# The last two feed-forward blocks get a second input X with the norm's factors in it, and wide up products from the third pair on

## The chip, the cores and the metric

The kernel runs on one core of one Trainium2 chip. The metric is device time in microseconds (us) of one execution of the whole program. TensorE (PE in the profile) multiplies, VectorE (DVE) and ScalarE (ACT) do elementwise work, GpSimd (POOL) sets a few pad columns to zero, SyncE (SP) issues the transfers of the weights.

## What is computed

Four transformer layers of width 1024 on one short sequence: two layers on 272 positions (16 of them meta tokens), then two on 256. Each layer is a mixer and a feed-forward block (FFN). The change is in the FFN of the last two layers:

```python
def conv_glu_ffn(xn, w_up, conv_w, w_down):
    u = causal_dwconv_2(xn @ w_up, conv_w)          # w_up: 1024 x 5632, 3 taps, each channel
    g, val = jnp.split(u, 2, axis=-1)               # 2816 gate channels, 2816 value channels
    return (jax.nn.silu(g) * val) @ w_down          # w_down: 2816 x 1024

def rms_norm_2(x, g):
    y = xf * lax.rsqrt(jnp.mean(xf * xf, axis=-1, keepdims=True) + EPS)
    return (y * g.astype(jnp.float32)).astype(x.dtype)

x = x + conv_glu_ffn(rms_norm_2(x, ffn_norm[l]), ffn_w_up[l], ffn_conv_w[l], ffn_w_down[l])
```

In the first two layers only the gate half goes through the convolution.

## The kernel before

Activations lie transposed: 128 channels on the partitions, positions (T = 256 here) along the free axis, so `hv[0..7]` hold the 1024 channels. A product in full float32 is made of three products of rounded float32 ("fp32r"): every operand is split into a high and a low part, and hi·hi, hi·lo and lo·hi are summed in PSUM. For the activations that split is done once for each norm (`X`: a tile with [high | low] side by side, 512 columns). For the weights it is done for each tile of 128x1024 as it arrives: ScalarE writes `whi` (L257), VectorE subtracts to get `wlo` (L258).

The norm is pulled apart. `X` holds only x times the gain g. The factor of each position, rB, comes later (`Norm.factors`: squares, sums, a reciprocal root on VectorE, and a broadcast through TensorE), so that products can start before it is known, and each output is multiplied by rB when it leaves PSUM.

An FFN walks over 11 pairs. A pair is two gate outputs (`evg`) and two value outputs (`evu`) of 128 channels each. I call each such output a unit: U1 to U44 in an FFN, U1 to U4 being the first pair. A unit has 8 steps along the 1024 input channels. `mm3` has two forms of a step:

```python
        if ps.shape[1] == 2 * n:
            mm(ps.rearrange("p (a n) -> p a n", a=2), w[0], x, start=first, stop=False)
        else:
            mm(ps, w[0], hi, start=first, stop=False)
            mm(ps, w[0], lo, start=False, stop=False)
        mm(ps[:, :n], w[1], hi, start=False, stop=last)
```

The narrow form is three products of 256 columns. The wide form is one of 512 (whi against [high | low]) and one of 256, and leaves two halves in the PSUM bank that must still be added. Before, the last two FFNs (`both=True`) use the narrow form in all of gate and up; `down` uses the wide one. The FFN of the second layer (`both=False`) already uses the wide form for its value outputs: there ScalarE copies one half out (L405) and VectorE adds the other (L406).

A unit of the last two FFNs is evicted in `conv3`: VectorE multiplies PSUM by rB into `gu` or `vu` (L382), ScalarE scales by the first tap (L385), VectorE adds the two others (L386, L387). A gate unit then goes through Silu (L396, ScalarE). For a value unit VectorE multiplies by the gate (L410, `a`), and the result is split for `down` (`ax`, L257 and L258). So VectorE has 3 instructions for every unit, 2 more for a value unit and one `wlo` for every unit: 20 for a pair of the walk.

Each engine runs its instructions in one fixed order, which the tile framework's scheduler decides when the program is built. So an instruction that waits holds up all that stand behind it on its engine. Three buffers bind the engines to each other: `whi` and `wlo` have 4 buffers each (a unit takes one of each), the PSUM tag `d` has 3 banks (U4 needs the bank of U1), and the raw weights have 2 buffers of two units.

`tick` runs twice a unit, and each time advances every chain that was started (the norm's factors are such a chain).

Of the kernel before, what the change touches and what calls it, by code (L numbers as in the profile page):

```python
# [11 lines left out]
F32 = mybir.dt.float32  # L12
F32R = mybir.dt.float32r
I32 = mybir.dt.int32
AF = mybir.ActivationFunctionType
OP = mybir.AluOpType
# [3 lines left out]
P = 128  # L20
D = 1024
KT = D // P
NMETA = 16
SEQ = 256
T1 = NMETA + SEQ
# [106 lines left out]
class Norm:  # L132
# [1 line left out]


    def __init__(self, k, hv, g, segs, delay):
        self.k, self.hv, self.segs, self.delay = k, hv, segs, delay
        V, A = k.nc.vector, k.nc.scalar
        T = hv[0].shape[1]
        self.X = []  # L140
        for t in range(KT):
            x = k.st.tile([P, 2, T1], F32R, tag=f"x{t}", name=f"x{t}")[:, :, :T]
            xh, xl = x[:, 0, :], x[:, 1, :]
            A.activation(xh, hv[t], AF.Copy, scale=g[:, t:t + 1])
            V.scalar_tensor_tensor(xl, hv[t], g[:, t:t + 1], xh.bitcast(F32), OP.mult, OP.subtract)
            self.X.append(x)
        self._u = self._r = self._rB = None
        self.chain = self.factors()
        k.start(self.chain)
# [36 lines left out]
    u = property(lambda self: self.have("_u"))  # L186
# [4 lines left out]
class K:  # L191
# [174 lines left out]
    def ffn(self, hv, N, lead, w_up, conv, w_down, both, done=None):  # L366

        nc, V, A = self.nc, self.nc.vector, self.nc.scalar
        X = N.X
        TX = X[0].shape[2]  # L370
        T = TX - lead
        XU = [x[:, :, lead:] for x in X]
        hv = [t[:, lead:] for t in hv]
        with self.tc.tile_pool(name="ffn", bufs=2) as fp:
            acts = []
            wide = 2 if 2 * T <= 512 and not both else 1

            def conv3(ps, c, tag):
                n = ps.shape[1]
                u = fp.tile([P, 2 + T1], F32, tag=tag + "u", name=tag + "u")  # L380
                nc.gpsimd.memset(u[:, 0:2], 0.0)
                V.tensor_tensor(u[:, 2:2 + n], ps, N.rB, OP.mult)  # L382
                o = n - T
                y = fp.tile([P, T1], F32, tag=tag + "y", name=tag + "y")[:, :T]
                A.activation(y, u[:, o:o + T], AF.Copy, scale=conv(0, c))  # L385
                V.scalar_tensor_tensor(y, u[:, o + 1:o + 1 + T], conv(1, c), y, OP.mult, OP.add)  # L386
                V.scalar_tensor_tensor(y, u[:, o + 2:o + 2 + T], conv(2, c), y, OP.mult, OP.add)  # L387
                return y

            for p in range(NF // 2):  # L390
                G = {}

                def evg(m, ps, p=p, G=G):
                    y = conv3(ps, 2 * p + m, "g")
                    s = fp.tile([P, T1], F32, tag=f"s{m}", name=f"s{m}")[:, :T]
                    A.activation(s, y, AF.Silu)  # L396
                    G[m] = s

                def evu(m, ps, p=p, G=G):
                    if both:  # L400
                        y = conv3(ps, NF + 2 * p + m, "v")
                    else:
                        y = fp.tile([P, T1], F32, tag="vy", name="vy")[:, :T]
                        if wide == 2:
                            A.activation(y, ps[:, T:], AF.Copy)  # L405
                            V.tensor_tensor(y, ps[:, :T], y, OP.add)  # L406
                            ps = y
                        V.tensor_tensor(y, ps, N.rB[:, lead:], OP.mult)
                    a = fp.tile([P, T1], F32, tag="a", name="a")[:, :T]
                    V.tensor_tensor(a, y, G[m], OP.mult)  # L410
                    c = 2 * p + m
                    x = fp.tile([P, 2, T1], F32R, tag=f"ax{c}", name=f"ax{c}", bufs=1)[:, :, :T]
                    self.split(x[:, 0, :], x[:, 1, :], a)
                    acts.append(x)

                self.dense(w_up[p], X, evg)
                self.dense(w_up[NF // 2 + p], XU, evu, wide=wide)
            w = [self.pieces(w_down[m2], NF) for m2 in range(D // 256)]
            ahead = [next(w[0]), next(w[0])]
            self.evict()  # L420
            for m2 in range(D // 256):
                def ev(m, ps, m2=m2):
                    k = 2 * m2 + m
                    for o in range(0, ps.shape[1], T):
                        V.tensor_tensor(hv[k], ps[:, o:o + T], hv[k], OP.add)
                    if done:
                        done(k)
                self.dense_pair(w[m2], acts, ev, "ns"[m2 % 2], () if m2 else ahead)
# [26 lines left out]
def mixer1(k_, l, h, N, final, first=None):  # L455
    nc, V, A, G = k_.nc, k_.nc.vector, k_.nc.scalar, k_.nc.gpsimd
    mm, tr = nc.tensor.matmul, nc.tensor.transpose
# [17 lines left out]
    def tmp(name):  # L475
        return mp.tile([P, T1 + 4], F32, tag="tmp", name=name, bufs=7)
# [109 lines left out]
    def ev_conv(which, c0):  # L586
        def ev(m, ps):
            hh = c0 + m
            ci = {"q": 0, "k": 4, "v": 8}[which] + hh
            xp = tmp("xp")  # L590
            G.memset(xp[:, 0:3], 0.0)
            V.tensor_tensor(xp[:, 3:3 + T], ps, N.rB, OP.mult)
# [1036 lines left out]
```

## Time and profile before

| | us |
|---|---|
| median of 3 runs (1605.9 to 1612.46) | 1608.96 |
| the profiled execution's own time | 1609.75 |
| its span, first to last instruction | 1607.9 |
| gate and up of the third FFN, from U1's first product (1027.18) to down's first (1153.68) | 126.5 |
| the same of the last FFN (1414.72 to 1542.04) | 127.3 |

The 1.9 us between the span and the execution's own time lie outside the profile. The profile has one execution; a row of a timeline gives the start, the duration, the engine, the line and the tiles. Durations on TensorE are longer than the step from one product to the next, since products overlap in the array, so its pace is read from starts. The same holds for VectorE and ScalarE to a smaller degree.

### The profile page before, as it was taken

The numbers are of one execution on the slowest core, as the hardware profiler recorded it, in microseconds if no ns is written. First come the engines' busy times: TensorE is split into PE (matmuls) and PEld (weight loads), VectorE is DVE, ScalarE is ACT, GpSimd is POOL, SyncE is SP. The second block draws the span as 40 slices with busy tenths as digits, with TensorE's granted clock in tenths as the row PEclk, the third lists the DMA queues.
The fourth block names the chain that finished last, engine by engine and source line by source line (L and its number), as shares of the span: only waits on it lengthen the run. The fifth ranks groups of instructions, "written<-read, shape, count | busy, mean of one in ns | idle before, by whom it ended". The sixth has DMA issues, their size and how long they took to land.

```text
span 1607.9 us, 29362 instructions
## 1 busy us (share of the span) xinstructions
PE 1587.6 (99%) x11482; PEld 1477.2 (92%) x11482; DVE 1247.1 (78%) x2729; ACT 897.4 (56%) x1582; POOL 16.1 (1%) x170
## 2 busy tenths in 40 slices
PE   7999999999999999999999999999999999999998
PEld 7988999999999989999998988999988888899997
DVE  7798678888558886788986659999866777789974
ACT  6566555555445755656665547666554444556642
POOL 0000000000000000000000000000000000000000
PEclk9999999999999999999999999999999999999999
DMA  6423234555553323355555653455555455555553
GB/s 209 156 80 131 78 133 164 178 172 171 167 187 131 105 79 108 105 187 179 185 185 187 218 169 120 161 196 188 184 176 197 157 160 171 167 183 184 184 193 121
DMA packets 38441, 257.71 MB, mean 160 GB/s; under 512 B 4384, under 2 KB 6816, under 8 KB 9120
## 3 DMA queue, kind: packets, MB, share of 16 engines
q1 hardware_dynamic: 37440, 253.66, 46.8%
q8 instruction: 90, 1.47, 0.4%
q10 hardware_dynamic: 864, 2.18, 0.4%
q14 instruction: 47, 0.39, 0.1%
HBM read 254.78 MB, written 1.05 MB: 159 GB/s over the span
## 4 chain that ended last, share of the span: by engine, by line
PE 93%; DVE 4%; ACT 2%; issue 0%; DMA 0%; DVEq 0%; SPq 0%; ACTq 0%
PE psd L285 19%; PE psd L283 18%; PE psd L284 18%; PE pss L281 5%; PE psn L281 5%; PE psd L281 3%; PE pss L285 3%; PE psn L285 3%; PE stat L496 1%; PE psd L348 1%; PE psd L349 1%; PE psd L350 1%; DVE wlo L258 1%; PE psn L349 1%; PE psn L348 1%; PE psn L350 1%
## 5 line engine op out<-in xcount | busy, mean ns | idle before, releaser
L257 ACT ACTIVATE whi<-raw 128x1024 fp32r<-128x1024 f32 (+1 forms) x487 | 508.4, 1045 | 535.0 <-PE psd L284 278.2
L258 DVE TENSOR_TENSOR wlo<-raw,whi 128x1024 fp32r<-128x1024 f32 (+1 forms) x487 | 585.7, 1203 | 207.6 <-ACT whi L257 202.4
L285 PE MATMUL psd<-x,wlo 128*128 128x256 f32 (+2 forms) x2384 | 683.4, 287 | 0.8 <-DVE wlo L258 0.8
L283 PE MATMUL psd<-x,whi 128*128 128x256 f32 (+2 forms) x2208 | 642.7, 292 | 7.6 <-ACT whi L257 6.9
L284 PE MATMUL psd<-x,whi 128*128 128x256 f32 (+2 forms) x2208 | 631.4, 286 | 0.0
L285 PEld LDWEIGHTS psd<-x,wlo 128*128 128x128 f32 x2384 | 452.3, 190 | 4.2 <-DVE wlo L258 1.6
L283 PEld LDWEIGHTS psd<-x,whi 128*128 128x128 f32 x2208 | 419.9, 190 | 15.5 <-ACT whi L257 6.9
L284 PEld LDWEIGHTS psd<-x,whi 128*128 128x128 f32 x2208 | 421.1, 191 | 3.3 <-issue 1.7
L285 PE MATMUL psn<-ax,wlo 128*128 128x256 f32 (+1 forms) x352 | 99.2, 282 | 0.0
L285 PE MATMUL pss<-ax,wlo 128*128 128x256 f32 (+1 forms) x352 | 99.2, 282 | 0.0
L281 PE MATMUL psn<-ax,whi 128*128 128x512 f32 x264 | 92.3, 392 | 0.0
L281 PE MATMUL pss<-ax,whi 128*128 128x512 f32 x264 | 92.2, 392 | 0.0
L285 PEld LDWEIGHTS psn<-ax,wlo 128*128 128x128 f32 x352 | 66.2, 188 | 0.0
L285 PEld LDWEIGHTS pss<-ax,wlo 128*128 128x128 f32 x352 | 66.2, 188 | 0.0
L281 PE MATMUL psd<-x,whi 128*128 128x512 f32 x176 | 61.7, 393 | 0.0
L281 PEld LDWEIGHTS pss<-ax,whi 128*128 128x128 f32 x264 | 49.5, 188 | 11.3
L281 PEld LDWEIGHTS psn<-ax,whi 128*128 128x128 f32 x264 | 49.5, 188 | 11.3
L385 ACT ACTIVATE gy<-gu,prm 128x256 f32<-128x256 f32 (+1 forms) x88 | 43.8, 502 | 4.0 <-DVE gu L382 3.7
L387 DVE SCALAR_TENSOR_TENSOR gy<-gu,prm,gy 128x256 f32<-128x256 f32 (+1 forms) x88 | 42.6, 487 | 1.7
L386 DVE SCALAR_TENSOR_TENSOR gy<-gu,prm,gy 128x256 f32<-128x256 f32 (+1 forms) x88 | 42.4, 485 | 0.9 <-ACT gy L385 0.9
L382 DVE TENSOR_TENSOR gu<-psd,rB 128x256 f32<-128x256 f32 (+2 forms) x88 | 37.1, 426 | 5.0 <-PE psd L285 3.7
L410 DVE TENSOR_TENSOR a<-vy,s 128x256 f32<-128x256 f32 (+1 forms) x88 | 37.5, 427 | 2.5 <-ACT s L396 0.5
(417 smaller groups left out, 2451.4 us busy)
## 6 DMA issues: line engine op xcount, KB each, us to landing
raw<-in_w_up_dram SPq DMA_DIRECT2D x44, 1024.0 KB, 4.8
raw<-in_ffn_w_up_dram SPq DMA_DIRECT2D x44, 1024.0 KB, 4.8
raw<-in_w_in_dram SPq DMA_DIRECT2D x26, 1024.0 KB, 4.8
raw<-in_w_gate_dram SPq DMA_DIRECT2D x16, 1024.0 KB, 4.9
raw<-in_w_down_dram SPq DMA_DIRECT2D x16, 1024.0 KB, 4.9
raw<-in_ffn_w_down_dram SPq DMA_DIRECT2D x16, 1024.0 KB, 4.9
raw<-in_even_w_in_dram SPq DMA_DIRECT2D x10, 1024.0 KB, 5.0
raw<-in_w_out_dram SPq DMA_DIRECT2D x8, 1024.0 KB, 4.8
```

What stands on the lines that cost most here:

```text
L257: self.nc.scalar.activation(hi, src, AF.Copy)
L258: self.nc.vector.tensor_tensor(lo, src, hi.bitcast(F32), OP.subtract)
L281: mm(ps.rearrange("p (a n) -> p a n", a=2), w[0], x, start=first, stop=False)
L283: mm(ps, w[0], hi, start=first, stop=False)
L284: mm(ps, w[0], lo, start=False, stop=False)
L285: mm(ps[:, :n], w[1], hi, start=False, stop=last)
L348: mm(ps[m], h, hi[:, k, :], start=(kk == 0), stop=False)
L382: V.tensor_tensor(u[:, 2:2 + n], ps, N.rB, OP.mult)
L385: A.activation(y, u[:, o:o + T], AF.Copy, scale=conv(0, c))
L386: V.scalar_tensor_tensor(y, u[:, o + 1:o + 1 + T], conv(1, c), y, OP.mult, OP.add)
L387: V.scalar_tensor_tensor(y, u[:, o + 2:o + 2 + T], conv(2, c), y, OP.mult, OP.add)
L410: V.tensor_tensor(a, y, G[m], OP.mult)
```

## The change

The FFN of the last two layers starts a chain of its own, `renorm`. As soon as rB is there, it makes a second input `XN` out of h: one VectorE instruction for each of the 8 channel tiles (x times gain times rB, `xny`, L406 of the changed kernel), and a split into [high | low] (`xn0` to `xn7`, ScalarE L257 and VectorE L258). From the first pair at whose start all 8 are there, all units of the FFN read `XN` in the wide form, and nothing is multiplied by rB at eviction: ScalarE copies one half out of PSUM into `u` (L386), VectorE adds the other half (L387). The first pairs stay as they were, at lines L389, L393, L394 and L436.

```diff
     def __init__(self, k, hv, g, segs, delay):
-        self.k, self.hv, self.segs, self.delay = k, hv, segs, delay
+        self.k, self.hv, self.g, self.segs, self.delay = k, hv, g, segs, delay
...
                 n = ps.shape[1]
+                if n > TX:
+                    n = TX
                 u = fp.tile([P, 2 + T1], F32, tag=tag + "u", name=tag + "u")
                 nc.gpsimd.memset(u[:, 0:2], 0.0)
-                V.tensor_tensor(u[:, 2:2 + n], ps, N.rB, OP.mult)
+                if ps.shape[1] > n:
+
+                    A.activation(u[:, 2:2 + n], ps[:, n:], AF.Copy)
+                    V.tensor_tensor(u[:, 2:2 + n], ps[:, :n], u[:, 2:2 + n], OP.add)
+                else:
+                    V.tensor_tensor(u[:, 2:2 + n], ps, N.rB, OP.mult)
...
+            XN = []
+
+            def renorm():
+
+                while N._rB is None:
+                    yield
+                for t in range(KT):
+                    x = fp.tile([P, 2, T1], F32R, tag=f"xn{t}", name=f"xn{t}", bufs=1)[:, :, :T]
+                    y = fp.tile([P, T1], F32, tag="xny", name="xny")[:, :T]
+                    V.scalar_tensor_tensor(y, hv[t], N.g[:, t:t + 1], N.rB, OP.mult, OP.mult)
+                    self.split(x[:, 0, :], x[:, 1, :], y)
+                    XN.append(x)
+                    yield
+
+            if both:
+                self.start(renorm())
             for p in range(NF // 2):
                 G = {}
+                if len(XN) == KT:
+                    X = XU = XN
+                    wide = 2
...
-                self.dense(w_up[p], X, evg)
+                self.dense(w_up[p], X, evg, wide=wide if both else 1)
                 self.dense(w_up[NF // 2 + p], XU, evu, wide=wide)
```

The program has 576 products fewer: 2 FFNs, 36 units each (U9 to U44), 8 steps, one product less in a step. Up to the arrival of rB in the third FFN, and again between the two FFNs, all engines' orders are the same as before.

Place one, VectorE in the last FFN around the arrival of rB. In the order before, `wlo_17097` is the low weights of U6, `wlo_17137` those of U7, and the three L382 are the first instructions that need rB (evictions of U1, U2 and U3):

```order
L258 TENSOR_TENSOR wlo_17097<-raw_17053,whi_17096 128x1024
L251 TENSOR_TENSOR nwt_b_16918<-nwt_a_16917,nrm_u_16914 128x2
L252 SCALAR_TENSOR_TENSOR nrm_y_16916<-nwt_b_16918,nrm_y_16916 128x2
L382 TENSOR_TENSOR gu_16963<-psd_16863,rB_16946 128x256
L382 TENSOR_TENSOR gu_17003<-psd_16933,rB_16946 128x256
L382 TENSOR_TENSOR vu_17041<-psd_16978,rB_16946 128x256
L258 TENSOR_TENSOR wlo_17137<-raw_17134,whi_17136 128x1024
```

The same place in the changed kernel, from U6's low weights (`wlo_16925`) on, and then, 22 rows further, the piece that ends with the low weights of U7 (`wlo_16965`) and U8 (`wlo_17003`):

```order
L258 TENSOR_TENSOR wlo_16925<-raw_16871,whi_16924 128x1024
L251 TENSOR_TENSOR nwt_b_16706<-nwt_a_16705,nrm_u_16702 128x2
L252 SCALAR_TENSOR_TENSOR nrm_y_16704<-nwt_b_16706,nrm_y_16704 128x2
L406 SCALAR_TENSOR_TENSOR xny_16740<-h0_69,norms_67,rB_16734 128x256
L389 TENSOR_TENSOR gu_16756<-psd_16651,rB_16734 128x256
L406 SCALAR_TENSOR_TENSOR xny_16766<-h1_70,norms_67,rB_16734 128x256
L389 TENSOR_TENSOR gu_16806<-psd_16721,rB_16734 128x256
L258 TENSOR_TENSOR xn0_16739<-xny_16740,xn0_16739 128x256
```

```order
L406 SCALAR_TENSOR_TENSOR xny_16920<-h7_76,norms_67,rB_16734 128x256
L394 SCALAR_TENSOR_TENSOR vy_16910<-vu_16907,prm2_11152,vy_16910 128x256
L389 TENSOR_TENSOR gu_16953<-psd_16877,rB_16734 128x256
L436 TENSOR_TENSOR a_16914<-vy_16910,s1_16813 128x256
L258 TENSOR_TENSOR xn7_16919<-xny_16920,xn7_16919 128x256
L393 SCALAR_TENSOR_TENSOR gy_16956<-gu_16953,prm2_11152,gy_16956 128x256
L258 TENSOR_TENSOR ax1_16916<-a_16914,ax1_16916 128x256
L394 SCALAR_TENSOR_TENSOR gy_16956<-gu_16953,prm2_11152,gy_16956 128x256
L258 TENSOR_TENSOR wlo_16965<-raw_16962,whi_16964 128x1024
L389 TENSOR_TENSOR gu_16993<-psd_16928,rB_16734 128x256
L258 TENSOR_TENSOR wlo_17003<-raw_16962,whi_17002 128x1024
```

U7's low weights stood 3 rows behind the arrival of rB, and now stand 35 rows behind it (18 SCALAR_TENSOR_TENSOR and 17 TENSOR_TENSOR of 128x256), all 16 rows of `xny` and `xn` ahead of them.

Place two, VectorE in the third FFN. Before, between the low weights of U7 (`wlo_12855`) and of U8 (`wlo_12893`):

```order
L258 TENSOR_TENSOR wlo_12855<-raw_12852,whi_12854 128x1024
L387 SCALAR_TENSOR_TENSOR gy_12724<-gu_12721,prm2_11152,gy_12724 128x256
L386 SCALAR_TENSOR_TENSOR vy_12762<-vu_12759,prm2_11152,vy_12762 128x256
L382 TENSOR_TENSOR vu_12802<-psd_12734,rB_12664 128x256
L387 SCALAR_TENSOR_TENSOR vy_12762<-vu_12759,prm2_11152,vy_12762 128x256
L410 TENSOR_TENSOR a_12766<-vy_12762,s0_12688 128x256
L258 TENSOR_TENSOR wlo_12893<-raw_12852,whi_12892 128x1024
```

In the changed kernel, the last rows before U8's low weights (`wlo_12933`):

```order
L406 SCALAR_TENSOR_TENSOR xny_12850<-h7_76,norms_67,rB_12664 128x256
L258 TENSOR_TENSOR ax0_12793<-a_12791,ax0_12793 128x256
L258 TENSOR_TENSOR xn6_12820<-xny_12821,xn6_12820 128x256
L436 TENSOR_TENSOR a_12844<-vy_12840,s1_12743 128x256
L258 TENSOR_TENSOR xn7_12849<-xny_12850,xn7_12849 128x256
L389 TENSOR_TENSOR gu_12883<-psd_12807,rB_12664 128x256
L258 TENSOR_TENSOR ax1_12846<-a_12844,ax1_12846 128x256
L389 TENSOR_TENSOR gu_12923<-psd_12858,rB_12664 128x256
L393 SCALAR_TENSOR_TENSOR gy_12886<-gu_12883,prm2_11152,gy_12886 128x256
L258 TENSOR_TENSOR wlo_12933<-raw_12892,whi_12932 128x1024
```

Behind the arrival of rB, U8's low weights now are the 37th VectorE row (17 SCALAR_TENSOR_TENSOR, 18 TENSOR_TENSOR, and two `wlo`, U7's being the 13th); before they were the 13th.

Place three, ScalarE in the wide units (here around U27 and U28 of the third FFN; `vu_13763` is U27's, `whi_13876` and `whi_13912` are the high weights of U32 and U33):

```order
L386 ACTIVATE vu_13763<-psd_13715 128x256
L257 ACTIVATE whi_13876<-raw_13843 128x1024
L422 ACTIVATE s1_13740<-gy_13736 128x256
L392 ACTIVATE vy_13767<-vu_13763,prm2_11152 128x256
L386 ACTIVATE vu_13799<-psd_13746 128x256
L257 ACTIVATE whi_13912<-raw_13910 128x1024
```

The copy out of PSUM (L386) is a new ScalarE row in each wide unit. VectorE's first instruction of an eviction, which waited for TensorE alone, now stands behind it.

## Rows read from the trace of the kernel before

**Rows 1.** The page: span, busy time of each engine, chain that ended last.
```profile
span 1607.9 us, 29362 instructions
PE 1587.6 (99%) x11482; PEld 1477.2 (92%) x11482; DVE 1247.1 (78%) x2729; ACT 897.4 (56%) x1582; POOL 16.1 (1%) x170
...
PE 93%; DVE 4%; ACT 2%; issue 0%; DMA 0%; DVEq 0%; SPq 0%; ACTq 0%
```
**Rows 2.** Stretch of the last FFN: PE, PEld, DVE, ACT, POOL busy, clock, DMA.
```profile
1482.00:1502.00 20.00, 20.00 (x171) 20.00 (x170) 18.94 (x35) 12.60 (x21) 0.70 (x7) 1.00 0.57 184
```
**Rows 3.** Timeline of ScalarE, third FFN: start, duration, engine, line, tiles, [idle].
```profile
1060.04 1.06 ACT L257 ACTIVATE whi<-raw 128x1024 fp32r<-128x1024 f32 x1 [1.07 <-PE psd L284]
...
1105.48 1.06 ACT L257 ACTIVATE whi<-raw 128x1024 fp32r<-128x1024 f32 x1 [0.81 <-PE psd L284]
```
**Rows 4.** Timeline of TensorE, second FFN: first wide product, next two narrow units.
```profile
755.29 0.39 PE L281 MATMUL psd<-x,whi 128*128 128x512 f32 x1
...
760.84 0.28 PE L283 MATMUL psd<-x,whi 128*128 128x260 f32 x1
...
766.58 0.39 PE L281 MATMUL psd<-x,whi 128*128 128x512 f32 x1
```
**Rows 5.** Timeline of VectorE, last FFN: the pace of its three kinds of instruction.
```profile
1428.74 0.48 DVE L386 SCALAR_TENSOR_TENSOR vy<-vu,prm,vy 128x256 f32<-128x256 f32 x1
1429.13 0.42 DVE L382 TENSOR_TENSOR vu<-psd,rB 128x256 f32<-128x256 f32 x1
1429.46 0.48 DVE L387 SCALAR_TENSOR_TENSOR vy<-vu,prm,vy 128x256 f32<-128x256 f32 x1
1429.86 1.22 DVE L258 TENSOR_TENSOR wlo<-raw,whi 128x1024 fp32r<-128x1024 f32 x1
1430.99 0.42 DVE L410 TENSOR_TENSOR a<-vy,s 128x256 f32<-128x256 f32 x1
```
**Rows 6.** Timeline of VectorE, both FFNs, from rB on.
```profile
1034.87 1.23 DVE L258 TENSOR_TENSOR wlo<-raw,whi 128x1024 fp32r<-128x1024 f32 x1 [0.71 <-ACT whi L257]
1036.01 0.75 DVE L382 TENSOR_TENSOR gu<-psd,rB 128x256 f32<-128x256 f32 x2
...
1425.02 0.76 DVE L382 TENSOR_TENSOR gu<-psd,rB 128x256 f32<-128x256 f32 x2 [1.28 <-ACT rB L178]
1425.69 0.42 DVE L382 TENSOR_TENSOR vu<-psd,rB 128x256 f32<-128x256 f32 x1
1426.02 1.22 DVE L258 TENSOR_TENSOR wlo<-raw,whi 128x1024 fp32r<-128x1024 f32 x1
```
**Rows 7.** Timeline of TensorE: down's first product in both FFNs, U4's in the last.
```profile
1153.68 0.39 PE L281 MATMUL psn<-ax,whi 128*128 128x512 f32 x1
...
1425.50 0.38 PE L283 MATMUL psd<-x,whi 128*128 128x256 f32 x1 [0.57 <-DVE gu L382]
...
1542.04 0.39 PE L281 MATMUL psn<-ax,whi 128*128 128x512 f32 x1
```
**Rows 8.** Second FFN's value units: the two instructions of a wide eviction, by tile.
```profile
L405 ACT ACTIVATE vy<-psd x21: 364/367/386, 735.7 to 849.8; 128x256 f32<-128x256 f32 x21
L406 DVE TENSOR_TENSOR vy<-psd,vy x20: 416/418/426, 736.6 to 842.6; 128x256 f32<-128x256 f32 x20
```
**Rows 9.** TensorE around waits: a product's wait, three stretches, products at half clock.
```profile
14.09 0.17 PE L496 MATMUL stat<-g,sqm 64*16 64x1 f32 x1 [1.86 <-ACT sqm L492]
...
14.00:22.00 8.00, 7.15 (x35) 6.66 (x35) 5.68 (x31) 2.12 (x5) 0.00 (x0) 0.57 0.68 251
1422.00:1432.00 10.00, 9.20 (x76) 8.81 (x76) 8.65 (x20) 5.45 (x11) 0.30 (x3) 1.00 0.32 105
...
604.00:610.00 6.00, 6.00 (x40) 5.96 (x40) 2.92 (x11) 3.58 (x13) 0.00 (x0) 0.72 0.52 178
...
606.69 0.42 PE L284 MATMUL psd<-x,whi 128*128 128x260 f32 x1
606.91 0.42 PE L285 MATMUL psd<-x,wlo 128*128 128x260 f32 x1
```

## The prediction, made before the changed kernel ran

> **What bounds the kernel now.** I read the page first. TensorE is busy for 99% of the span, and 93% of the chain that ended last is its products [rows 1]. So time is won where a product becomes shorter or fewer, and lost where TensorE has to wait. Then I read the stretches of the two FFNs that change. In 20 us of gate and up TensorE never rests at full clock, VectorE is busy for 18.94 us and ScalarE for 12.60 [rows 2]. VectorE is the engine to watch: it has about 1.06 us to spare in 20, some 0.6 in a pair of the walk, and everything that is put on it in a hurry comes on top of nearly full work. Next I needed the pace of TensorE, and that I took from starts that are far apart. ScalarE takes up the weights of a new unit each time that TensorE is done with an old one; 16 units lie between the two rows, 45.44 us, 2.84 us for a narrow unit [rows 3]. The second FFN has wide units of 256 positions already: two of them take 760.84 - 755.29 = 5.55 us, 2.776 each, and the two narrow ones behind them, of 260 columns, take 5.74 [rows 4]. Last I read the waits at the arrival of rB. There TensorE waits 0.57 us for an eviction in the last FFN before U4 [rows 7], and otherwise hardly in either FFN.
>
> **Step 1, the wide products.** 36 units in each FFN, 72 in all, go from 2.84 to 2.776 us: 72 x 0.064 = 4.6 us won. It is so little since the number of columns stays the same (768 in a step); what goes is one weight load and the fixed part of one product. The lower bound is from the narrow units beside the wide ones: 5.74 us less the four extra columns (4/260 of it, 0.09) is 5.65, so 0.05 a unit and 3.6 us in all. I take 4.6, as it is measured in the very units that change.
>
> The Trainium skill bears on this, in "TensorE: Matmul & The Clock Gate", section "Back-to-back issue gap": a product alone takes N/2.4 + 2.5 ns at full clock. By that, a step of three narrow products takes 327.5 ns, the wide one 325.0, and the 576 steps win 1.4 us, an estimate from that page of the Trainium skill, and the sum below would end at 1616.4. The rows give 355 ns (2.84/8) and 347, so here a product's fixed part is several times what the Trainium skill states, and the sum goes by the rows.
>
> **Step 2, what VectorE has to do at eviction.** L387 (PSUM plus SBUF) stands where L382 (PSUM times SBUF) stood. In the second FFN the same addition takes 418 ns [rows 8], the old product 0.42 us [rows 5], so nothing changes on VectorE. On ScalarE a copy of 367 ns [rows 8] comes in for each wide unit. Its work of 12.60/20 x 2.84 = 1.79 us a unit becomes 2.16 of 2.78: hidden, and ScalarE has room. By starts, VectorE's instructions take 0.39 or 0.40 (SCALAR_TENSOR_TENSOR), 0.33 (TENSOR_TENSOR) and 1.13 us (`wlo`) [rows 5]. A pair has 8, 8 and 4 of them: 3.16 + 2.68 + 4.52 = 10.4 us, against 11.36 now and 11.1 in wide units. So 0.7 us a pair may go on waits for ScalarE's copy before VectorE becomes the bound. In place three of the order other VectorE work lies between evictions, so I take zero; what it costs otherwise is a rival below.
>
> **Step 3, the second X, last FFN.** `renorm` adds 8 of the 0.395 and 8 of the 0.335 us to VectorE, 5.84 us in each FFN, and 8 short ScalarE activations, which ScalarE hides. What they cost depends on what stands behind them. Before, three evictions follow the arrival of rB at 1425.02, and U7's low weights start at 1426.02 [rows 6]. Now 35 rows stand ahead of them (place one): 18 x 0.395 + 17 x 0.335 = 12.8 us. With `wlo` itself (1.22 to its last element) U7's low weights are there at 1425.02 + 12.8 + 1.2 = 1439.0. When does TensorE want them? Down starts at 1542.04, 41 units after U4's start [rows 7]: 41 x 2.84 = 116.4, so U4 starts at 1425.6, which agrees with the row at 1425.50. The first `xny` stands ahead of U1's eviction, whose bank U4 needs, so U4 starts 0.4 later than now: +0.4. U7 then starts at 1425.9 + 3 x 2.84 = 1434.4. It can do two products with its high weights, and the order puts two of U8 beside them (0.47 us in all); then it stands until 1439.0. That is 4.1 us of waiting, with 0.4 from U4 4.5 us. Behind it nothing is late: VectorE finishes U8's low weights 1.5 us further, while U7 needs 2.7.
>
> **Step 4, the second X, third FFN.** U8 starts 37 units ahead of down: 1153.68 - 37 x 2.84 = 1048.6 [rows 7]. From 1036.01, when rB is used first [rows 6], to U8's low weights there are 17 x 0.395 + 18 x 0.335 + 2 x 1.13 = 15.0 us (place two), so they end at 1051.1. TensorE does three products meanwhile (two of U8, one wide one of U9, 0.47 us): 2.0 us of waiting, in pieces. U7's low weights (13th row) are there before 1042, and U7 starts at 1045.8, so no wait there. Bounds for steps 3 and 4 together: nothing, if the waits found other cover, and the whole 5.84 us in each FFN, 11.7, if none of the new work found a gap. I take the 6.5 of the laid-out rows.
>
> **Step 5, the clock.** A wait of TensorE has an aftermath in this trace. After a product that waited 1.86 us the granted clock is 0.57 on average from 14 to 22 us, after thin work it is 0.72 from 604 to 610 [rows 9]; the levels are 1.2 and 2.4 GHz, so the lower one held for (1 - 0.57) x 8/0.5 = 6.9 us and for 3.4 us. At the lower level a product of 260 columns takes 0.215 us [rows 9] and at full clock 5.74/48 = 0.12 [rows 4], so such a fall loses 44% of its length: 3.0 or 1.5 us. The wait of 0.57 us before U4 [rows 7] left the clock at 1.00 [rows 9]. The 4.1 us of step 3 are more than twice the 1.86, so I expect the clock to fall once, and take the short fall, since dense products follow: 1.5 us. The 2.0 us of step 4 come in pieces with products between; I take no fall there. Bounds: zero, and two long falls, 6.0.
>
> **The sum.** -4.6 + 4.5 + 2.0 + 1.5 = +3.4 us on the profiled execution's 1609.75: 1613.2. The median of the runs is 0.8 lower, 1608.96, so I say 1613 for the time. Within 0.5% (8 us, about what a measurement of this kernel can tell from no change) this is the same time, on the slow side.
>
> **Rivals.**
> 1. *The waits are covered.* VectorE's instructions would have to run closer than they do, or TensorE's look-ahead would have to be deeper than the 4 weight buffers. Against it stands the fixed order of place one. Then only step 1 is left: 1605 us. Chance 0.13.
> 2. *VectorE becomes the bound in the wide units* (L387 waits for ScalarE's copy, which can stand behind a `whi` of 1.06 us [rows 3]). The point is 0.7 us of waits in a pair. If it takes back all that step 1 gives, the time is 1617.8; with 1.4 us of waits a pair, 18 pairs lose 13 us against the forecast, 1626. For it: 18.94 of 20 us [rows 2]. Against it: the second FFN, where the same pair of instructions in half of the units keeps them at 2.776, though with two VectorE instructions fewer in a pair of the walk. Chance 0.10, and this is the case that ends slower.
> 3. *The clock falls twice, or long.* One more short fall gives 1614.7, two long ones 1617.7. Chance 0.22.
> 4. *The missing product wins little.* If nearly all of a product's time is its columns, the 0.064 us a unit [rows 3, 4] come from elsewhere in the second FFN and only a part shows up here: between nothing and 3.6 us, so 1614.2 to 1617.8, with 1616 in the middle. Against it: both paces stand in rows of the same core and clock. Chance 0.05. (The estimate from the Trainium skill in step 1, page "TensorE: Matmul & The Clock Gate", lies inside that span.)
> 5. *The wide form comes later than the third pair, or not at all*: excluded by the order, which has 576 products fewer.
>
> **How the numbers follow.** The forecast has 0.48, with 1610.5 to 1615.5 as its own range (the waits 1.5 us either way, one fall of 0 to 3.0). The rest, 0.02, is what I have not thought of. The range has to take in most of rivals 1 and 3 and the near half of 2: 1606 to 1620. For slower by more than 0.5% (above 1617.0) I count 0.07 of rival 2, 0.09 of rival 3 and 0.05 of the forecast's own tail: 0.21. Faster by more than 0.5% (below 1600.9) needs 8 us, where step 1 alone gives 4.6: 0.03. The same: 0.76.
>
> **What would show it.** Step 1: in the changed kernel's last pairs two starts of ScalarE's `whi` 16 units apart lie 44.4 us apart, not 45.44. Step 3: in the last FFN one product of L285 waits about 2 to 4 us for VectorE's `wlo`, with down's first product late by the wait less 2.3 us. Step 4: the same some 12 us behind rB in the third FFN, about half as long. Step 5: clock under 1.00 in the stretch behind the long wait and nowhere else new. Step 2: VectorE's idle time before L387 under 0.7 us a pair. I am wrong if TensorE waits for L387, if the long wait is not there, or if wide units in these FFNs are not at 2.78 us.

## The result, and the profile after

The changed kernel takes 1621.7 us (median of 5 runs, 1616.79 to 1626.45), against 1608.96 for the kernel before on the same chip (5 runs, 1605.9 to 1612.46). The ratio is 1.0061, with a 95% interval of 1.0041 to 1.0081: slower by 7 to 13 us. A second set of runs later (C2 below) gave 1619.31 against 1611.6 us, ratio 1.0053 (1.0036 to 1.0071). I had forecast 1613 and a range up to 1620; the median lies 1.7 us above that range, and above the 1617.0 up to which I had called it the same time.

The page of the changed kernel: span, busy time and instructions of each engine, chain that ended last, and the two groups of wide products in the units.

```profile
span 1624.7 us, 28328 instructions
...
PE 1598.5 (98%) x10906; PEld 1459.4 (90%) x10906; DVE 1256.9 (77%) x2761; ACT 924.6 (57%) x1670; POOL 16.1 (1%) x170
...
PE 92%; DVE 5%; ACT 2%; DMA 1%; issue 1%; DVEq 0%; SPq 0%; ACTq 0%
...
L281 PE MATMUL psd<-xn,whi 128*128 128x512 f32 x576 | 201.4, 393 | 0.2 <-DVE gu L389 0.2
L285 PE MATMUL psd<-xn,wlo 128*128 128x256 f32 x576 | 160.8, 279 | 0.0
```

TensorE has 576 products fewer than in [rows 1], and the span is still longer. VectorE's share of the chain that ended last went from 4% to 5%.

The next three views show where TensorE waits. First its timeline in the third FFN, only the rows with a wait (start, duration, line, tiles, idle time before and what ended it):

```profile
1058.85 0.36 PE L283 MATMUL psd<-x,whi 128*128 128x256 f32 x1 [0.54 <-DVE gu L389]
1059.51 0.47 PE L281 MATMUL psd<-xn,whi 128*128 128x512 f32 x1 [0.20 <-DVE gu L389]
1061.03 0.39 PE L285 MATMUL psd<-x,wlo 128*128 128x256 f32 x1 [1.05 <-DVE wlo L258]
```

The same in the last FFN: U4's first product, U8's first product, and U7's first product with low weights.

```profile
1436.63 0.39 PE L283 MATMUL psd<-x,whi 128*128 128x256 f32 x1 [0.97 <-DVE gu L389]
...
1447.18 0.36 PE L283 MATMUL psd<-x,whi 128*128 128x256 f32 x1 [1.53 <-DVE gu L389]
...
1450.10 0.58 PE L285 MATMUL psd<-x,wlo 128*128 128x256 f32 x1 [2.45 <-DVE wlo L258]
1450.48 0.41 PE L283 MATMUL psd<-x,whi 128*128 128x256 f32 x1
```

VectorE at the same place: the first row that uses rB, and U7's low weights.

```profile
1435.75 0.48 DVE L406 SCALAR_TENSOR_TENSOR xny<-h,norms,rB 128x256 f32<-128x256 f32 x1 [1.28 <-ACT rB L178]
...
1448.82 1.22 DVE L258 TENSOR_TENSOR wlo<-raw,whi 128x1024 fp32r<-128x1024 f32 x1
```

U7's low weights start 13.07 us behind the arrival of rB, where it was 1.00 us before [rows 6]. VectorE has no gap in between (the stretch, its busy time, instructions, granted clock, DMA share, GB/s):

```profile
1435.75:1448.82 13.07, 13.04 (x35) 1.00 0.19 78
```

U4's wait grew from 0.57 [rows 7] to 0.97, and around U7, where nothing waited before, TensorE now stands idle twice. The order puts U8's first two products between U7's two with high weights and U7's first with low weights. U8 needs the PSUM bank of U5, whose eviction (the L389 at the end of the 1.53 us) is late in VectorE's queue, and then U7 needs its low weights (2.45 us). The last row of TensorE's block shows the aftermath: the product behind the wait takes 0.41 us instead of 0.28. The windows of TensorE around it (busy time, products, granted clock, DMA share, GB/s):

```profile
1446.00:1448.00 2.00, 0.47 (x2) 1.00 0.00 0
1448.00:1450.00 2.00, 0.00 (x0) 0.71 0.00 0
1450.00:1452.00 2.00, 1.90 (x9) 0.50 0.00 0
1452.00:1454.00 2.00, 2.00 (x11) 0.50 0.59 168
1454.00:1456.00 2.00, 2.00 (x12) 0.58 0.84 356
1456.00:1458.00 2.00, 2.00 (x19) 1.00 0.33 45
```

The clock falls to the lower level while TensorE stands, and stays there through 5.6 us of dense products. Behind the waits of the third FFN it stays at 1.00.

Last, the pace of the wide units, from ScalarE's timeline in the last pairs (19 units lie between the two rows), and VectorE's first instruction of a wide eviction, by groups, from 1470 to 1558 us:

```profile
1505.49 1.06 ACT L257 ACTIVATE whi<-raw 128x1024 fp32r<-128x1024 f32 x1 [0.66 <-PE psd L281]
...
1558.53 1.06 ACT L257 ACTIVATE whi<-raw 128x1024 fp32r<-128x1024 f32 x1 [0.72 <-PE psd L281]
```
```profile
L387 DVE TENSOR_TENSOR gu<-psd,gu 128x256 f32<-128x256 f32 x16 | 6.7, 421 | 0.0
L387 DVE TENSOR_TENSOR vu<-psd,vu 128x256 f32<-128x256 f32 x15 | 6.3, 420 | 0.0
```

A wide unit takes 53.04/19 = 2.792 us, not the 2.776 of the sum, and VectorE is not idle before L387 at all.

**A way to compare that is finer than the times.** The third FFN's first product started at 1027.18 us in the profile of before and at 1036.73 after. Up to there the two programs have the same orders, so these 9.55 us are not an effect of the rows that the change moves. They go with the clock: ahead of that product the clock records of the traces have 44.4 us at the lower level after and 23.9 us before, and over all 14 profiles of the table the start moves by 0.46 us for each us at the lower level (20.5 x 0.46 = 9.4). I therefore compare profiles from that product on: to down's first product of the third FFN ("third"), on to the last FFN's first product ("between"), to its down's first product ("last"), and to the end ("tail"). "Whole" is the sum, "against" its difference from 580.7; the ratio is that of the runs, with its interval.

| kernel | starts at | third | between | last | tail | whole | against | ratio of the runs |
|---|---|---|---|---|---|---|---|---|
| before | 1027.18 | 126.50 | 261.04 | 127.32 | 65.86 | 580.72 | | |
| C1, before again | 1023.65 | 126.50 | 260.99 | 127.30 | 65.86 | 580.65 | | |
| after | 1036.73 | 127.35 | 261.38 | 132.99 | 66.25 | 587.97 | +7.3 | 1.0061 (1.0041 to 1.0081) |
| C2, after again | 1029.13 | 127.34 | 261.35 | 132.77 | 66.21 | 587.67 | +7.0 | 1.0053 (1.0036 to 1.0071) |
| E1, second X, not used | 1031.99 | 129.19 | 261.04 | 133.94 | 65.94 | 590.11 | +9.4 | 1.0069 (1.0049 to 1.0089) |
| E2, wide, no second X | 1031.81 | 125.05 | 261.33 | 125.88 | 66.23 | 578.49 | -2.2 | 0.9987 (0.9971 to 1.0002) |
| E3, half the pace | 1028.20 | 127.54 | 261.25 | 132.45 | 65.96 | 587.20 | +6.5 | 1.0040 (1.0020 to 1.0060) |
| E4, rB product on GpSimd | 1030.65 | 127.82 | 261.34 | 130.75 | 65.74 | 585.65 | +4.9 | 1.0031 (1.0017 to 1.0045) |
| E5, all of it off VectorE | 1031.42 | 129.20 | 261.89 | 128.83 | 65.46 | 585.38 | +4.7 | 1.0027 (1.0012 to 1.0043) |
| E6, rB at eviction, GpSimd | 1032.44 | 135.71 | 261.36 | 135.21 | 65.78 | 598.06 | +17.4 | 1.0108 (1.0086 to 1.0130) |
| E7, products in the waits | 1028.40 | 127.36 | 261.34 | 130.48 | 66.22 | 585.40 | +4.7 | 1.0034 (1.0018 to 1.0050) |
| E8, half of the second X | 1032.01 | 126.51 | 261.03 | 127.69 | 65.86 | 581.09 | +0.4 | 1.0001 (0.9988 to 1.0015) |
| E9, rB at eviction, VectorE | 1032.55 | 127.85 | 266.22 | 130.22 | 71.76 | 596.05 | +15.3 | one run, 1630.35 us |
| E10, a quarter of the pace | 1033.72 | 125.54 | 261.69 | 128.73 | 65.92 | 581.88 | +1.2 | 0.9989 (0.9976 to 1.0002) |

Two profiles of one kernel agree within 0.3 us in "whole", while their starts differ by 3.5 and 7.6 us. And "against", divided by 1610, lies inside the interval of the measured ratio in every row that has one but E10's (+7.0 us is 1.0043, +17.4 is 1.0108; E10's +1.2 is 1.0007, above its 1.0002). So the change costs about 7 us.

### The profile page after: what moved, and what is told of

Its sections match the earlier page's. It is cut to its first block, busy times and chain, and to the rows that moved or that the text cites. A ratio compares the mean times of both kernels' runs of the same rounds, so it can differ in the third digit from the quotient of the medians.

```text
span 1624.7 us, 28328 instructions
## 1 busy us (share of the span) xinstructions
PE 1598.5 (98%) x10906; PEld 1459.4 (90%) x10906; DVE 1256.9 (77%) x2761; ACT 924.6 (57%) x1670; POOL 16.1 (1%) x170
## 3 DMA queue, kind: packets, MB, share of 16 engines
q10 hardware_dynamic: 864, 2.18, 0.3%
HBM read 254.78 MB, written 1.05 MB: 157 GB/s over the span
## 4 chain that ended last, share of the span: by engine, by line
PE 92%; DVE 5%; ACT 2%; DMA 1%; issue 1%; DVEq 0%; SPq 0%; ACTq 0%
PE psd L285 19%; PE psd L283 14%; PE psd L284 13%; PE psd L281 11%; PE pss L281 5%; PE psn L281 5%; PE psn L285 3%; PE pss L285 3%; DVE wlo L258 1%; PE stat L522 1%; PE psd L348 1%; PE psd L349 1%; PE psd L350 1%; PE psn L349 1%; PE psn L348 1%; PE psn L350 1%
## 5 line engine op out<-in xcount | busy, mean ns | idle before, releaser
L257 ACT ACTIVATE whi<-raw 128x1024 fp32r<-128x1024 f32 (+1 forms) x487 | 508.0, 1045 | 488.4 <-PE psd L284 199.7
L258 DVE TENSOR_TENSOR wlo<-raw,whi 128x1024 fp32r<-128x1024 f32 (+1 forms) x487 | 585.5, 1203 | 205.2 <-ACT whi L257 198.5
L285 PE MATMUL psd<-x,wlo 128*128 128x272 f32 (+2 forms) x1808 | 524.5, 291 | 3.6 <-DVE wlo L258 3.5
L283 PE MATMUL psd<-x,whi 128*128 128x272 f32 (+2 forms) x1632 | 485.2, 298 | 11.0 <-ACT whi L257 6.6
L284 PE MATMUL psd<-x,whi 128*128 128x272 f32 (+2 forms) x1632 | 473.9, 291 | 0.0
L285 PEld LDWEIGHTS psd<-x,wlo 128*128 128x128 f32 x1808 | 347.6, 193 | 7.3 <-DVE wlo L258 4.6
L283 PEld LDWEIGHTS psd<-x,whi 128*128 128x128 f32 x1632 | 314.9, 193 | 20.4 <-ACT whi L257 6.9
L284 PEld LDWEIGHTS psd<-x,whi 128*128 128x128 f32 x1632 | 316.3, 194 | 3.3 <-issue 1.7
L281 PE MATMUL psd<-xn,whi 128*128 128x512 f32 x576 | 201.4, 393 | 0.2 <-DVE gu L389 0.2
L285 PE MATMUL psd<-xn,wlo 128*128 128x256 f32 x576 | 160.8, 279 | 0.0
L281 PEld LDWEIGHTS psd<-xn,whi 128*128 128x128 f32 x576 | 108.0, 188 | 25.5 <-issue 0.4
L285 PEld LDWEIGHTS psd<-xn,wlo 128*128 128x128 f32 x576 | 108.2, 188 | 0.0
L392 ACT ACTIVATE gy<-gu,prm 128x256 f32<-128x256 f32 (+1 forms) x88 | 44.4, 507 | 8.5 <-DVE gu L389 4.8
```

Source lines behind the costliest of these rows:

```text
L257: self.nc.scalar.activation(hi, src, AF.Copy)
L258: self.nc.vector.tensor_tensor(lo, src, hi.bitcast(F32), OP.subtract)
```

## The experiments

My theory was that of steps 3 to 5: VectorE's burst behind rB puts the weight splits late, TensorE waits for them, and its clock falls. The rivals: the wide form or its eviction costs; or the second X costs in whatever way it is made. All experiments are short edits of the changed kernel. **A correction to the expectations**: those of E3, E4, E5, E8 and E10 count 16 tiles of the second X and 11.7 us of VectorE work in each FFN. There are 8 tiles and 5.84 us (step 3 of the prediction has it right). E4 takes 8 rows of each FFN off VectorE. E8 computes 4 of 8 tiles (2.9 us). E3 lasts 10 units and leaves 32 wide ones in each FFN, as E5 does; E10 lasts 18 units, not 34, and leaves 24. What tells the theories apart is unchanged.

**E1 and E2: each half of the change alone.**

```diff
# E1
-                if len(XN) == KT:
+                if len(XN) > KT:
# E2
-            if both:
-                self.start(renorm())
...
-                if len(XN) == KT:
-                    X = XU = XN
+                if both and p >= 2:
                     wide = 2
```

> The second X is computed in the third and last FFN as in the changed kernel, but nobody uses it: all up products stay 3 x 256 columns and the factor rB is applied at eviction as before. If the burst of VectorE work behind rB is what costs (it puts the splits of the weights of U7 to U9 late, and TensorE's clock then falls), all of the cost stays and the small gain goes: third FFN +2.3 us of waits, last FFN +0.4 at U4 and about +4 at U7 with a clock fall of about 2.5 us behind it, together +9 us over the kernel before, ratio 1.004 to 1.007. If instead the wide products or their eviction are what costs, this kernel equals the kernel before (ratio 1.000, within 0.001) and no wait for wlo stands at U7.

> No second X: from the third pair on the up products of the third and last FFN use the raw X in the wide form (512 and 256 columns), with the wide eviction and no factor at all, so the factor rB is left out of U9 to U44. If the burst of VectorE work is the whole cost, this one is faster than the kernel before by 72 wide units times 0.048 us = 3.5 us (ratio about 0.998) and TensorE waits nowhere in either FFN from U5 on. If the wide form or its eviction costs (ScalarE's copy ahead of VectorE's add), it is slower than the kernel before by some us, with waits of TensorE for the eviction in the wide units.

E2 leaves the factor rB out of U9 to U44, so only its time is of use. E1 lost 9.4 us ("against"), E2 won 2.2; together that is 7.2, what the change costs. In E2 TensorE waits nowhere in either FFN from U5 on. E1's waits are at the same two products as in the changed kernel (U8's first, and U7's first with low weights):

```profile
1443.91 0.36 PE L283 MATMUL psd<-x,whi 128*128 128x256 f32 x1 [1.51 <-DVE gu L389]
1447.11 0.58 PE L285 MATMUL psd<-x,wlo 128*128 128x256 f32 x1 [2.73 <-DVE wlo L258]
```

Its clock falls too, but for a shorter time: the two windows below give 3.4 us at the lower level, where those of the changed kernel gave 6.8, though the wait ahead of it is the longer one.

```profile
1446.00:1450.00 4.00, 2.89 (x13) 0.63 0.27 37
1450.00:1454.00 4.00, 4.00 (x34) 0.94 0.54 229
```

So all of the cost is the second X, and the wide form with its eviction is a gain: 1.45 and 1.44 us in the two stages. Of this 0.3 us is given back between the FFNs and 0.4 in the tail.

**E8: half of the burst.** As E1, with `range(KT // 2)` in `renorm`.

> As the run that computes the second X and never uses it, but only 8 of its 16 tiles: half of the extra VectorE work (about 5.9 us instead of 11.7 in each FFN), just as bunched behind rB. If VectorE can be put some 6 to 7 us late before TensorE waits, the waits at U7 and in the third FFN vanish, the clock stays at 1.00, and the time is that of the kernel before: ratio 0.999 to 1.002. If each row of VectorE that goes ahead of the splits costs its share, half of the 9 us stays: ratio 1.002 to 1.004, with some 2 us of wait at U7 and a clock fall.

Nothing is left of the waits at U7 and in the third FFN. TensorE's list of waits from 1000 us on (line, what it waited for, us in total, times, longest):

```profile
PE psd L283 <- DVE gu L389: 1.0, 1, 1.0
PE psx L1451 <- DVE on L1442: 0.5, 1, 0.5
PE pss L362 <- DVE nrm_y L252: 0.2, 1, 0.2
PE psd L281 <- DVE ax L258: 0.2, 1, 0.2
```

Only U4's 0.4 us more stays, as in step 3. The cost is not proportional to the rows: 8 more rows of 128x256 in each FFN cost 0.4 us in the two together, 16 more cost 9.4 (E1). An estimate by the prediction's own arithmetic fits: U7 starts 9.4 us behind rB (1434.4 - 1425.0). In the order of this kernel 17 rows stand between rB and U7's low weights instead of 35; at some 0.365 us each, and 1.2 for the split, the weights are there after 7.4 us (7.7 by the trace), 2 us early, where 35 rows put them 4.6 us late.

**E7: keep TensorE busy in the waits.** In U7 of the last FFN 13 products go ahead of the first, and 20 behind the two that need no low weights:

```diff
+                    for _ in range(13):
+                        self.nc.tensor.matmul(self.fill[:, :T], w[0][0][:, 0, m:m + P], two(X[0])[0], start=True, stop=True)
...
+                        for _ in range(20):
+                            mm(self.fill[:, :T], hi, xh, start=True, stop=True)
```

> The changed kernel, with 33 products of 256 columns into a bank that nobody reads, ahead of and inside U7 of the last FFN, where TensorE waits 1.5 and 2.45 us. If the clock falls because TensorE waits there, the clock stays at 1.00 through U7 and U8 and the second half of the run (from the third FFN's down products to the end) is 2 to 2.5 us shorter than in the changed kernel (294.2 us from the first product of the second layer to the last FFN's first down product becomes 291.7 to 292.2); the waits themselves stay. If the fall has another cause, the clock falls all the same and the 294.2 us stay or grow.

TensorE's timeline there (the third row is U7's first product with low weights), and its windows:

```profile
1436.88 1.71 PE L305 MATMUL psx<-x,whi 128*128 128x256 f32 x13
...
1438.66 2.55 PE L314 MATMUL psx<-x,whi 128*128 128x256 f32 x20
...
1441.71 0.39 PE L315 MATMUL psd<-x,wlo 128*128 128x256 f32 x1 [0.26 <-DVE wlo L259]
```
```profile
1437.00:1439.00 2.00, 2.00 (x19) 1.00 0.00 0
1439.00:1441.00 2.00, 2.00 (x19) 1.00 0.00 0
1441.00:1443.00 2.00, 1.74 (x15) 1.00 0.00 0
1443.00:1445.00 2.00, 2.00 (x20) 1.00 0.37 66
```

U7's low weights come no earlier, the clock stays at 1.00, and the last FFN's stage is 130.48 us instead of 132.77 and 132.99: the fall costs 2.3 to 2.5 us. That is shown, not only argued, since from the third FFN on the order of all other instructions is the same.

**E3 and E10: the same work, spread out.** Four ticks later, and one tile for every two (E3) or four (E10) ticks. The diff is that of E10; E3 has `range(2)` in the second loop:

```diff
+                for _ in range(4):
+                    yield
                 for t in range(KT):
...
-                    yield
+                    for _ in range(4):
+                        yield
```

> The second X is computed four ticks later and at half the pace (one tile of it for every unit of the up loop instead of two), so the wide form begins about 12 units later. If the burst is the cost, the wait for wlo at U7 shrinks from 2.45 us to under 1, TensorE's clock stays at 1.00 there, some 24 wide units per FFN are left (2 x 24 x 0.048 = 2.3 us gained), and the time lies between 2 us below and 2 us above the kernel before (ratio 0.999 to 1.001). If it is the amount of VectorE work and not its bunching that costs, the waits only move some units later and the ratio stays near 1.004 to 1.006.

> The second X four ticks later and at a quarter of the pace (one tile for two units), so that only some 5 to 9 wide units are left in each FFN. VectorE has about 0.18 us to spare for a unit, so that 34 units take up about 6 of the 11.7 us: if the amount of VectorE work against its spare time sets the wait, the waits fall from 4.9 to under 1.5 us in the last FFN and the clock stays up: ratio 0.999 to 1.002. If the second X costs by another way, the waits only come later and the ratio is 1.003 or more.

E3 missed: it still lost 6.5 us. Its last FFN has waits of 0.44 and 2.02 us for `wlo` and 1.64 us for `whi` behind U4's, spread over 16 us, and a clock fall behind the last. E10 has one, 45 us behind U4's, without a fall:

```profile
1477.32 0.39 PE L285 MATMUL psd<-x,wlo 128*128 128x256 f32 x1 [1.15 <-DVE wlo L258]
```

So it is not enough to move the burst away from rB. An estimate fits both: VectorE, with 18.94 of 20 us busy [rows 2], gets rid of 5.84 us only at some 0.18 us a unit (the 0.7 us of step 2 in a pair, over 4 units). Over E3's 10 units that is 1.8 us, and some 4 are left over; over E10's 18 units it is 3.2, and the 2.6 left are near E8's 2.9, which cost next to nothing. E10 comes to 1.2 us over the kernel before by its profile, and to a ratio of 0.9989 by its runs: no difference from before that can be measured.

**E4 and E5: take the work off VectorE.** E4 puts the product with rB on GpSimd and the gain into ScalarE's copy; E5 puts the low part on GpSimd too, at E3's pace without its delay:

```diff
# E5
-                    V.scalar_tensor_tensor(y, hv[t], N.g[:, t:t + 1], N.rB, OP.mult, OP.mult)
-                    self.split(x[:, 0, :], x[:, 1, :], y)
+                    nc.gpsimd.tensor_tensor(y, hv[t], N.rB, OP.mult)
+                    A.activation(y, y, AF.Copy, scale=N.g[:, t:t + 1])
+                    A.activation(x[:, 0, :], y, AF.Copy)
+                    nc.gpsimd.tensor_tensor(x[:, 1, :], y, x[:, 0, :].bitcast(F32), OP.subtract)
```

> The product with rB of the second X goes from VectorE to GpSimd and the product with g to ScalarE's copy; VectorE keeps one instruction for a tile instead of two (16 fewer rows in the burst of each FFN, about 16 x 0.39 = 6 us less). If the length of the burst sets the wait, the 2.45 us at U7 vanish or fall below 0.5, with no clock fall: ratio about 0.999 to 1.001. If GpSimd is slow, tiles of the second X come one after another at its pace, the VectorE rows wait for it in the queue ahead of the splits, and the wait at U7 stays or grows: ratio 1.005 or more.

> All of the second X goes to GpSimd (product with rB, subtraction of the high part) and ScalarE (product with g, high part), at half the pace, one tile for each unit: VectorE has no row for it. About 24 wide units per FFN are left. If what costs is the amount of work that VectorE gets, in a stage where it is busy nearly all the time (11.7 us more in each of the two FFNs), both waits behind rB vanish and the time is 2 x 24 x 0.048 = 2.3 us under the kernel before: ratio 0.997 to 1.0005. If the cost is in the second X as such (its tiles come late, ScalarE's queue is held up), waits for xn, whi or s stand in its place: ratio 1.003 or more.

Both missed. TensorE waits 1.04 and 1.23 us in E4's third FFN and 1.82 and 0.90 in its last. E5 has no VectorE row of the second X, and TensorE still waits 1.72 us (third FFN) and 1.61 (last) for `wlo`. The reason is in VectorE's groups. First C1 (the kernel before), 1424 to 1454 us; the mean ns of one is the figure ahead of the second bar:

```profile
L258 DVE TENSOR_TENSOR wlo<-raw,whi 128x1024 fp32r<-128x1024 f32 x10 | 12.2, 1221 | 0.4 <-ACT whi L257 0.2
L386 DVE SCALAR_TENSOR_TENSOR gy<-gu,prm,gy 128x256 f32<-128x256 f32 x7 | 3.3, 478 | 0.0
...
L258 DVE TENSOR_TENSOR ax<-a,ax 128x256 fp32r<-128x256 f32 x6 | 2.5, 420 | 0.3 <-ACT ax L257 0.3
...
L382 DVE TENSOR_TENSOR gu<-psd,rB 128x256 f32<-128x256 f32 x6 | 2.5, 418 | 0.0
```

The same in E5, 1435 to 1465 us, and GpSimd's new rows:

```profile
L258 DVE TENSOR_TENSOR wlo<-raw,whi 128x1024 fp32r<-128x1024 f32 x8 | 10.8, 1356 | 0.1
L393 DVE SCALAR_TENSOR_TENSOR gy<-gu,prm,gy 128x256 f32<-128x256 f32 x6 | 4.3, 718 | 0.0
...
L258 DVE TENSOR_TENSOR ax<-a,ax 128x256 fp32r<-128x256 f32 x4 | 2.8, 689 | 0.0
...
L389 DVE TENSOR_TENSOR gu<-psd,rB 128x256 f32<-128x256 f32 x4 | 1.7, 416 | 0.0
```
```profile
L409 POOL TENSOR_TENSOR xn<-xny,xn 128x256 fp32r<-128x256 f32 x8 | 7.6, 949 | 2.5 <-ACT xn L408 2.5
L406 POOL TENSOR_TENSOR xny<-h,rB 128x256 f32<-128x256 f32 x6 | 4.8, 801 | 0.4
```

While GpSimd works, VectorE's instructions with two operands in SBUF get longer (478 to 718, 420 to 689, 1221 to 1356 ns), and that with an operand in PSUM does not (418 and 416). The Trainium skill names this, in "GPSIMD Engine Reference", section "1. Specifications": GpSimd's SBUF interfaces are shared with VectorE, with contention for VectorE instructions that have two SBUF inputs; the trace agrees. The work went off VectorE's queue and came back as its time.

**E6 and E9: no second X, rB behind the wide eviction** (as E2, with one more line in `conv3`; E9 has `V` for `nc.gpsimd`):

```diff
                     V.tensor_tensor(u[:, 2:2 + n], ps[:, :n], u[:, 2:2 + n], OP.add)
+                    nc.gpsimd.tensor_tensor(u[:, 2:2 + n], u[:, 2:2 + n], N.rB, OP.mult)
```

> No second X at all: the raw X goes in the wide form from the third pair on, and the factor rB is applied behind the eviction, by one product on GpSimd for each unit (0.93 us there by the profile of the run that has the same product). 72 wide units: 2.7 us of gain in the two FFNs as in the run without any factor, if GpSimd is off the path: ratio 0.997 to 1.000. If GpSimd's 0.93 us or its sharing with VectorE slows the evictions, TensorE waits for them and the ratio is over 1.003.

> No second X: raw X in the wide form from the third pair on, and VectorE multiplies by rB behind the eviction, four more instructions of 0.335 us for a pair. If VectorE has 0.7 us to spare in a pair, it is 0.6 us too long there, TensorE waits for the evictions, and the two FFNs are 18 x 0.6 = 11 us longer less the 2.7 us that the wide form wins: some 8 us over the kernel before in the stage times. If it has more to spare, the stage times are those of the run without any factor (125.05 and 287.06 us).

Both are the slowest of all, +17.4 and +15.3 us. In E6 TensorE waits 14 times for L387 of a gate unit (6.5 us in all) and 8 times for that of a value unit (4.3 us), the second rival's picture. E9 tests the slack: four instructions of 0.335 us more in a pair are too much. TensorE waits 8.7 us for `wlo`, and VectorE is so far behind at the end of each FFN that "between" and "tail" grow by 5.2 and 5.9 us. The expectation had 8 us for E9 in the two stages. They took 4.3 more than before, and the rest came where I had not looked: VectorE carries its backlog into `down`.

**C1 and C2: both kernels once more.**

> The kernel before once more, for a second profile of it. The runs so far lie 1605 to 1617 us apart. If chance falls of TensorE's clock in the mixers explain the spread, the two FFNs take the same times as in the first profile (126.5 us from the third FFN's first up product to its first down product, within 0.2), the start of the third FFN moves by some us from 1027.18, and the number of 10 us stretches with a clock under 1.00 moves with it.

> The changed kernel once more. Its two FFNs and what lies behind them were 6.7 us longer than in the kernel before (127.35, 294.17 and 66.25 us against 126.50, 288.34 and 65.86), while its median was about 10 us above. If the rest is chance in the part ahead of the third FFN, which the change does not touch, this ratio comes out at 1.003 to 1.006, with the same stage times within 0.5 us; if the change costs something there too, it stays at 1.006 or more.

Both came out as the table shows. Two windows of the mixers, of C1 and then of the changed kernel's first profile (PE, PEld, DVE, ACT, POOL busy, granted clock, DMA):

```profile
560.00:580.00 20.00, 18.62 (x121) 14.63 (x120) 18.99 (x71) 11.39 (x26) 0.20 (x2) 1.00 0.16 54
...
930.00:950.00 20.00, 20.00 (x113) 16.82 (x112) 9.94 (x13) 8.46 (x13) 0.20 (x2) 1.00 0.41 137
```
```profile
560.00:580.00 20.00, 18.89 (x108) 16.12 (x108) 16.71 (x76) 7.68 (x18) 0.10 (x1) 0.74 0.17 54
...
930.00:950.00 20.00, 20.00 (x147) 18.84 (x148) 12.36 (x30) 10.66 (x20) 0.30 (x3) 0.93 0.47 159
```

In the first profile of before the window at 560 has a clock of 0.83, in C1 1.00: such falls differ between executions of one kernel. What stays open: at 930 to 950 the clock was 1.00 in both profiles of before and under 1.00 in all twelve others, one fall of 3.4 us each, which adds 1.5 us. If that came in every run of a changed program and in none of before, the ratios would lie 0.0009 above what the stages behind it give. On average over the eleven ratios of the table they lie 0.0002 above it, and those of E2 and E8 within 0.0002.

## Why the prediction was right and wrong, by its steps

**Step 1** failed in size. I took 4.6 us from units of 2.776 us, which come two at a time between narrow ones in the second FFN [rows 4]. In a row of wide units it is 2.792, which gives 72 x 0.048 = 3.5 us, next to my lower bound of 3.6; E2 shows 2.9 us in the two stages (0.040 a unit) and 2.2 in the whole. The estimate of 1.4 us from the Trainium skill ("TensorE: Matmul & The Clock Gate", section "Back-to-back issue gap") lay below that; E2's whole is between it and mine.

**Step 2** held: VectorE is not idle ahead of L387 in the 88 us shown, and TensorE waits nowhere for L387.

**Step 3** held: VectorE's 35 rows took 13.07 us (said 12.8), U4 is 0.40 later (said 0.4), and by the starts of the products the two waits around U7 cost 1.69 + 2.61 = 4.3 us (said 4.1). I had laid it on one wait, for the low weights; it came as two, since the bank for U8's first products was late too.

**Step 4** held: waits of 0.54, 0.20 and 1.05 us, which by the starts of the products cost 0.70 + 0.35 + 1.29 = 2.3 us (said 2.0), in pieces, with no fall of the clock. The stage is 2.3 us longer than E2's, too.

**Step 5** failed in size: one fall, as said, but the longer of the two that I had rows for. 5.6 us of products at half pace, 2.3 to 2.5 us by E7, where I took 1.5.

**The sum** by what was measured: -2.2 + 4.7 + 2.3 + 2.4 = +7.2, and the two profiles show +7.0 and +7.3; I had +3.4. Of the 3.8 us that I missed, 2.4 are step 1 and 0.9 step 5. On the profiled execution of before +7.2 is 1617. The median of 1621.7 lies another 5 us up. In the profiles such differences lie ahead of the third FFN, where the clock falls differ (1036.73 in the first profile of the changed kernel, 1029.13 in the second); for the runs without a profile that is not shown. I had three runs of before, 6.6 us apart; 29 runs in the first series spread from 1605.27 to 1616.91. The range should have taken that in: its upper end of 1620 leaves 3 us above 1617, and the chance of slower (0.21) was too small. I put the range together from the costs of the change alone.

Of the rivals, the first did not come, and the second came only in E6 and E9. The third came in part: one long fall, 0.9 us more than I took. The fourth came in part and was the larger share: the missing product won 1.7 to 2.4 us less than I took.

## What to carry to other kernels

On an engine that is busy for 95% of a stage, added work is paid back at the rate of its slack (here an estimated 0.18 us a unit), so one asks how late the next thing in its queue may be, and not how long the work is: 2.9 us in each FFN cost 0.4 in the two together, 5.8 us cost 4.7 in one FFN and 2.3 in the other, plus the clock. A wait of TensorE can have a further price behind it, in the lower clock (2.4 us behind 4.3 us of waiting in the last FFN), but not each wait here had one. And where the executions of one kernel lie 10 us apart, two profiles compared from a common instruction on resolve 0.3 us, which the times could not.

## What the runs showed of the hardware that I had not expected

- GpSimd's products of 128x256 in SBUF take 0.80 to 0.95 us and lengthen VectorE's instructions with two SBUF operands beside them by 11 to 64% (E5), so moving elementwise work there from a full VectorE, at half the pace, won only some 2.4 us of 7.
- The lower clock came behind waits of 1.53 and 2.45 us in the changed kernel's last FFN, of 1.51 and 2.73 (E1), of 2.02 (E3), of 1.82 and 0.90 (E4) and of 0.65 and 1.72 (E5, third FFN). It did not come behind 0.54, 0.20 and 1.05 in the third FFN, behind E10's 1.15, behind 1.04 and 1.23 (E4, third FFN), behind 1.61 (E5, last FFN), behind 1.64 (E3), nor behind 2.18 us in E6's third FFN. There TensorE's wait, and then the stretch around it (busy time, products, granted clock, DMA share, GB/s), are:

```profile
1131.11 0.50 PE L281 MATMUL psd<-x,whi 128*128 128x512 f32 x1 [2.18 <-DVE gu L387]
```
```profile
1128.00:1138.00 10.00, 7.82 (x44) 1.00 0.50 156
```

  So the length of a wait does not decide by itself whether the clock falls, and E1 beside the changed kernel shows the same for how long it stays down.
- A wide step in `down` takes 17.42 us for 50 in the kernel before and in E1, E8 and E10, 17.43 in E3 and E5, and 17.51 or 17.50 in the changed kernel, E2, E4, E6 and E7. The line, the shapes and the full clock are the same, and the 0.3 us given back in "between" is this (176 steps). It is not the wide form as such, since E3, E5 and E10 have wide units too. I did not find the cause.
